# Layer 0's attention and MLP modulation on ScalarE and GpSimd instead of in 32-column strips of TensorE

## The chip, the core and the metric

The kernel runs on one NeuronCore of a Trainium2 chip. A core has engines that run side by side, each through its own instructions in a fixed order: TensorE (PE in the profile, its weight loads PEld), VectorE (DVE), ScalarE (ACT), GpSimd (POOL), and SyncE (SP), which here issues nearly all DMA transfers. The metric is the device time of one launch in microseconds.

## The reference, cut to what matters

Two layers work on 512 latent tokens and 256 context tokens of width 1024. Each layer makes six modulation vectors of 1024 numbers for the latent tokens (from the condition `c`) and six for the context tokens (from `c_ctx`), with one matrix of 1024 x 6144 for each layer.

```python
def modulation(cond, w_mod, b_mod):
    m = jax.nn.silu(cond) @ w_mod + b_mod
    return m.reshape(m.shape[:-1] + (N_MOD, D_MODEL))
...
for l in range(DEPTH):                       # DEPTH = 2
    sh1, sc1, ga1, sh2, sc2, ga2 = modulation(c, w_mod[l], b_mod[l])       # latent
    csh1, ... , cga2             = modulation(c_ctx, w_mod[l], b_mod[l])   # context
    h = modulate(rmsnorm(x, norm1_g[l]), sh1, sc1)
    z = h @ w_in[l]                          # q, k, v, u, g
    attn = softmax(q k^T) v ;  gm = gelu(u) * (w_s @ layernorm(gelu(g)) + b_s)
    x = x + ga1 * (concat(attn, gm) @ w_out[l])
    x = x + ga2 * (square(relu(modulate(rmsnorm(x, norm2_g[l]), sh2, sc2) @ w_ff1[l])) @ w_ff2[l])
```

The context stream does the same with its own vectors, but in the last layer only its keys and values are needed. So of layer 1 the context needs only the first two vectors (shift and scale of the first norm).

## The kernel before, in words

All numbers are float32. Large products are made of three matmuls on rounded halves: `split` (L206) makes `hi` on ACT and the rest `lo` as source minus `hi` on DVE or POOL, and each product takes hi x hi, hi x lo and lo x hi. The activations lie feature-major in units `A0..A7`, `B0..B6`, `C0`, `C1`, weights come as blocks of 128 x 1024 in a ring that SP loads ahead (`pump`, L224, four blocks live).

The 6144 modulation columns of a layer are 12 chunks `j` of 512 columns: chunks 0 to 3 are shift and scale of the first norm, 4 and 5 the gate of the output projection, 6 to 9 shift and scale of the second norm, 10 and 11 the gate of the MLP. Two ways of making a chunk exist:

- `mod_chunk` (L315): eight float32 matmuls of 32 x 512 (L326), whose results stand in four 32-row strips of a PSUM bank `pb`. DVE turns the bank in 32 x 32 blocks (L334), and four small matmuls with a selection matrix (L339) add the strips. Layer 0 uses it for all its chunks: 0 to 3 at the start, 4 to 11 in the attention. Its weights go through the common ring (tile `hi`).
- `mod_wide` (L347): for each of 8 rows of blocks, and for both conditions, ACT multiplies 128 x 512 weights by a number for each partition (L368, into a tile `s`), and POOL adds the product to an accumulator (L369, two inputs in SBUF). After eight rows DVE turns (L380) and sums (L381) the accumulators, and four small matmuls (L386) finish. Layer 1's chunks are made so while layer 0's MLP runs. The weights come through two buffers of the tile `k`.

Tiles `s` are shared: the ring `tsm` (L184) has three buffers for products, for GELU's work tiles, for squares and for others.

One emission clock (`Flow`, L48) counts TensorE time in ns while the program is written: `defer` puts work off to a time of this clock, `fill` and `step` put in pieces of filler. A scheduler then orders each engine's instructions by its own estimate, except in regions marked as written by hand (the start on PE and DVE, layer 0's MLP on DVE and ACT).

A layer runs: projections of u, g, k, v and q (`PLAN`, L116), attention, output projection, second norm, MLP. In a projection each PSUM bank is drained by ACT and DVE: `qk` (L588) squares on ACT, multiplies by the rotary tables on DVE (L597, L601, PSUM in), adds (L602), makes 1/rms in nine small DVE instructions (L277 to L287) and scales (L608). `stack` splits the result (L613 on ACT, L614 on POOL for layer 0). In attention a tile of 128 queries takes scores on PE (`pa<-B,B`, L203), a maximum on DVE (L825), the exponential on ACT (L828), a reciprocal on DVE (L830), a copy on POOL (L833), turns on PE (L844), halves on ACT and DVE (L846, L847) and the product with V on PE (`pb<-A,B`). After each of layer 0's 48 tiles one piece of filler is emitted: first the eight pieces of chunks 4 and 5, then, as `FILL0` (L114) says, 16 pieces of the output projection of the gated half (o, `pb<-A,hi`) and 24 pieces of chunks 6 to 11 (m). `make_gm` (L770) must have split that half before (L774 on ACT, L775 on DVE for two tiles and on POOL for two).

## Time and profile before

| | |
|---|---|
| median of 3 runs | 1533.01 us (1531.71 to 1535.66) |
| span of the profiled execution | 1530.9 us, from the first to the last instruction; 2.1 us less than the median of the runs, which stands for its own time, as the profiled execution's whole time is not given apart |
| PE busy | 1484.1 us, 97% |
| DVE, ACT, POOL busy | 957.4, 682.6, 402.0 us |
| instructions | 22786 |

On this time axis layer 0's projections lie at 42 to 177 us, its attention at 177 to 351, its MLP at 436 to 905, layer 1 behind. A row of the view by stretches gives, for each engine, busy time and number of instructions, then granted clock of TensorE, share of the DMA engines and GB/s. In a row of groups stand busy us and mean ns of one, then the idle time of the engine just before, with what ended it. A profile's fp32 matmul counts as two or more records, so a strip matmul is two.

### The profile page before, as it was taken

The page shows a single profiled execution, that of the slowest core. Times are in us where ns is not written, and L with a number is a line of the kernel's source. Part 1 is how long each engine was busy: PE and PEld are TensorE (multiplying, and loading weights), DVE is VectorE, ACT ScalarE, POOL GpSimd, SP SyncE. Part 2 cuts the span into 40 slices and gives each one's busy share as a digit, 9 for nine tenths or more (in the row PEclk, how much of TensorE's full clock was granted, in tenths as well). Part 3 has the DMA queues.
Part 4 walks back from the last instruction along what each step waited for, and adds up shares of the span by engine and source line. Part 5 has one row for each costly group of instructions (what it writes and reads, how often), then busy time and mean ns, then how long its engine had stood idle before and what let it go on. Part 6 is the DMA issues. An engine that isn't in the chain of part 4 may idle for free.

```text
span 1530.9 us, 22786 instructions
## 1 busy us (share of the span) xinstructions
PE 1484.1 (97%) x8804; PEld 1321.5 (86%) x8804; DVE 957.4 (63%) x1874; ACT 682.6 (45%) x1142; POOL 402.0 (26%) x362
## 2 busy tenths in 40 slices
PE   6999899999999999999999999998999999999998
PEld 2899686779899999999999998996889888888887
DVE  5868966776855555555555547988796644444443
ACT  3542355564545453545444424535784433322221
POOL 0112320023244545545454603035213000000000
PEclk9999999999999999999999999999999999999999
DMA  9221324321134333333333321221101333332332
GB/s 359 67 74 48 119 91 152 110 83 56 62 108 122 113 123 126 111 118 106 124 109 124 98 68 56 86 80 44 41 1 56 97 96 97 98 97 97 96 98 79
DMA packets 49948, 148.83 MB, mean 97 GB/s; under 512 B 5424, under 2 KB 6832, under 8 KB 49840
## 3 DMA queue, kind: packets, MB, share of 16 engines
q1 hardware_dynamic: 49264, 146.46, 29.9%
q8 instruction: 69, 1.13, 0.3%
q10 hardware_dynamic: 576, 0.92, 0.2%
q14 instruction: 39, 0.32, 0.1%
HBM read 145.26 MB, written 2.10 MB: 96 GB/s over the span
## 4 chain that ended last, share of the span: by engine, by line
PE 82%; DVE 12%; DMA 2%; ACT 2%; issue 1%; POOL 0%; SPq 0%; ACTq 0%; POOLq 0%; DVEq 0%
PE pa L203 51%; PE pb L203 21%; PE pt L844 3%; PE pt L203 3%; PE pb L326 2%; DVE lo L208 1%; DMA X<-in_xT 1%; DMA C<-in_w_mod 1%; DVE X L784 1%; DMA A<-in_w_mod 1%; DVE m L277 1%; PE pt L626 1%; DVE B L961 1%; ACT hi L207 1%; PE pb L865 0%
## 5 line engine op out<-in xcount | busy, mean ns | idle before, releaser
L203 PE MATMUL pa<-A,hi 128*128 128x384 f32 (+2 forms) x1696 | 449.2, 347 | 1.7 <-ACT w L954 0.6
L207 ACT CAST hi<-raw 128x1024 fp32r<-128x1024 f32 x171 | 179.5, 1050 | 409.9 <-PE pa L203 326.3
L208 DVE TENSOR_TENSOR lo<-raw,hi 128x1024 fp32r<-128x1024 f32 x155 | 202.7, 1308 | 215.8 <-ACT hi L207 212.4
L203 PEld LDWEIGHTS pa<-A,hi 128*128 128x128 f32 x1696 | 304.7, 188 | 25.9 <-ACT w L954 1.8
L369 POOL TENSOR_TENSOR C<-C,s 128x512 f32<-128x512 f32 x168 | 240.5, 1463 | 245.0 <-ACT s L368 244.8
L203 PE MATMUL pa<-A,lo 128*128 128x384 f32 (+2 forms) x848 | 293.4, 347 | 1.1 <-DVE lo L208 1.1
L203 PE MATMUL pa<-B,hi 128*128 128x384 f32 (+1 forms) x900 | 246.4, 356 | 4.4 <-DVE X L784 4.4
L203 PEld LDWEIGHTS pa<-B,hi 128*128 128x128 f32 x900 | 162.9, 188 | 21.5 <-DVE X L784 9.2
L784 DVE SCALAR_TENSOR_TENSOR X<-pa,modT,X 128x384 f32<-128x384 f32 (+1 forms) x168 | 88.0, 547 | 143.0 <-PE pa L203 143.0
L203 PEld LDWEIGHTS pa<-A,lo 128*128 128x128 f32 x848 | 159.3, 188 | 12.0 <-DVE lo L208 1.3
L203 PE MATMUL pa<-B,lo 128*128 128x384 f32 (+1 forms) x450 | 158.1, 353 | 0.0
L203 PE MATMUL pb<-B,hi 128*128 128x256 f32 (+2 forms) x600 | 152.3, 340 | 0.4 <-DVE X L784 0.4
L368 ACT ACTIVATE s<-k,silu 128x512 f32<-128x512 f32 x168 | 114.3, 716 | 49.4 <-DMA k<-in_w_mod 27.3
L203 PE MATMUL pb<-hi,A 128*128 128x256 f32 x672 | 126.1, 285 | 0.0
L784 DVE SCALAR_TENSOR_TENSOR X<-pb,modT,X 128x512 f32<-128x512 f32 (+3 forms) x116 | 69.1, 602 | 75.8 <-PE pb L203 75.3
L203 PEld LDWEIGHTS pb<-B,hi 128*128 128x128 f32 x600 | 104.0, 189 | 11.6 <-DVE X L784 1.0
L203 PEld LDWEIGHTS pb<-hi,A 128*128 128x128 f32 x672 | 106.1, 191 | 0.2 <-issue 0.2
L203 PE MATMUL pb<-B,lo 128*128 128x256 f32 (+2 forms) x300 | 101.5, 338 | 0.0
L203 PE MATMUL pb<-lo,A 128*128 128x256 f32 x336 | 95.3, 284 | 0.0
L203 PEld LDWEIGHTS pa<-B,lo 128*128 128x128 f32 x450 | 84.4, 188 | 5.8
L847 DVE TENSOR_TENSOR A<-pt,A 128x384 fp32r<-128x384 f32 (+1 forms) x144 | 73.6, 535 | 16.4 <-ACT A L846 14.4
L846 ACT CAST A<-pt 128x384 fp32r<-128x384 f32 (+1 forms) x144 | 64.6, 469 | 43.3 <-PE pt L844 39.5
(169 smaller groups left out, 2300.3 us busy)
## 6 DMA issues: line engine op xcount, KB each, us to landing
raw<-in_w_ff SPq DMA_DIRECT2D x128, 512.0 KB, 3.5
k<-in_w_mod SPq DMA_DIRECT2D x96, 256.0 KB, 3.0
hi<-in_w_mod SPq DMA_DIRECT2D x32, 512.0 KB, 3.6
raw<-in_w_tok SPq DMA_DIRECT2D x19, 512.0 KB, 3.5
raw<-in_w_out SPq DMA_DIRECT2D x16, 512.0 KB, 3.5
A<-in_w_mod SPq DMA_DIRECT2D x8, 512.0 KB, 9.9
raw<-in_w_u SPq DMA_DIRECT2D x8, 512.0 KB, 3.5
B<-in_w_mod SPq DMA_DIRECT2D x6, 512.0 KB, 10.2
```

The costliest lines, as they stand in the source:

```text
L203: pe.matmul(out, a, b, start=start, stop=stop)
L207: act.copy(hi, src)
L208: (eng or vec).tensor_tensor(out=lo, in0=src, in1=hi.bitcast(F32), op=ALU.subtract)
L277: vec.tensor_scalar(yi, v.bitcast(I32), -0.5, 1595932665.0, op0=ALU.mult, op1=ALU.add)
L326: pe.matmul(ps[q:q + 32, :], S32[:, k, :], w[:, k2 * 512:(k2 + 1) * 512], start=k < ns, stop=k >= KT - ns)
L368: act.activation(p, w, AF.Copy, scale=s)
L369: pool_e.tensor_tensor(out=a, in0=a, in1=p, op=ALU.add)
L626: pe.transpose(p[:, o:o + 128], stk[:, t, hh, c0:c0 + 128].bitcast(F32), ident)
L784: vec.scalar_tensor_tensor(out=xs, in0=src[:, s - off:e - off], scalar=modT[l][:, i * 8 + m, cond:cond + 1], in1=xs, op0=ALU.mult, op1=ALU ...
L844: pe.transpose(tp_[:, (kt - k0) * 128:(kt - k0) * 128 + 128], p[:, kt * 128:kt * 128 + 128], ident)
L846: act.copy(pth[:, k0:k0 + step, d], src)
L847: vec.tensor_tensor(out=ptl[:, k0:k0 + step, d], in0=src, in1=pth[:, k0:k0 + step, d].bitcast(F32), op=ALU.subtract)
```

## The change

Chunks 4 to 11 of layer 0 are no longer made by `mod_chunk` but by `mod_wide`, as a background generator that the emission clock advances by one row of blocks for every 3600 ns of its time, from the start of layer 0's projections. `mod_wide` gets four buffers for the weights of its own (`mr`, three loaded ahead) and an accumulator of its own (`macc`); it gives up its turn after every row, and no longer between the last sum and the turning. For layer 1 the chunks 4 to 11 are made for the latent condition alone. `FILL0` now tells after which of the 48 attention tiles a piece of output projection is emitted. The lines of the changed kernel stand ten lower than before (L193 for L203, L198 for L208), and `mod_wide`'s are L345 (load), L361 (product), L362 (sum), L371 and L372 (turn, sum).

```diff
@@ PAR
-       "PV1": 9800.0, "NC": 21600.0, "REL": 4100.0, "NP": 14, ...
+       "PV1": 9800.0, "NC": 21600.0, "REL": 4100.0, "BG": 3600.0, "NP": 14, ...
@@ Flow.tick
         while self.todo and self.todo[0][0] <= self.vt:
             self.todo.pop(0)[2]()
+        while self.bg is not None and self.bgt <= self.vt:
+            self.bgt += next(self.bg, 1e9)
-FILL0 = "oooooooommmommmmmmmmmommmmommmommmomoomo"
+FILL0 = "1101101101101101" + "01000100010001000100100100100100"
@@ block_order: the blocks of chunks 4 to 11 leave the common stream
-        if l == 0:
-            o += mod(4) + mod(5)
...
+        o += [("out", l, w, nb) for w in range(2) for nb in range(4)]
@@ mod_wide
-        raw = tk([128, 2, 512], F32)
+        raws = [const.tile([128, 512], F32, tag=f"mr{i}", name=nm("mr")) for i in range(4)] if not mraw else mraw
...
+        for i in range(3):
+            load(i)
+        for i, (j, k) in enumerate(steps):
+            conds = range(2 if l == 0 or j < 4 else 1)
+            if k == 0:
+                acc = const.tile([128, 2, 512], F32, tag="macc", name=nm("macc"))
+            load(i + 3)
+            w = mraw[i % 4]
+            for cond in conds:
+                a, s = acc[:, cond, :], sc[:, k, cond:cond + 1]
+                if k == 0:
+                    act.activation(a, w, AF.Copy, scale=s)
+                else:
+                    p = tsm([128, 512])
+                    act.activation(p, w, AF.Copy, scale=s)
+                    pool_e.tensor_tensor(out=a, in0=a, in1=p, op=ALU.add)
+            if k < KT - 1:
+                yield period
+                continue
...
@@ attention
-                                fl.step()
+                                if FILL0[nt[0]] == "1":
+                                    fl.step()
+                                nt[0] += 1
...
-                fl.fillers = [mods((4, 5)), mixed(fl.fillers[0], mods((6, 7, 8, 9, 10, 11))), fl.fillers[1]]
@@ main
+    fl.bg, fl.bgt = mod_wide(0, range(4, 12), PAR["BG"]), fl.vt
```

The order of the instructions moves as follows at three places.

POOL, in layer 0's q projections. `C` is the gate path that takes the mixed values (L743, L738 in the new kernel), `k` the low half of a stacked query (L614, L609), `A` the low half of the gated values, `macc` an accumulator of a chunk, `lo` the low half of output weights. Before:

```order
L743 TENSOR_TENSOR C_125_566<-s_1663,C_125_566 128x2x256
L614 TENSOR_TENSOR k_1769<-w_1617,k_1769 128x8x64
L743 TENSOR_TENSOR C_125_566<-s_1753,C_125_566 128x2x256
L614 TENSOR_TENSOR k_1857<-w_1707,k_1857 128x8x64
L614 TENSOR_TENSOR k_1947<-w_1800,k_1947 128x8x64
L614 TENSOR_TENSOR k_2035<-w_1890,k_2035 128x8x64
L775 TENSOR_TENSOR A_418_2375<-C_125_566,A_418_2375 128x768
```

Now, from the second of these rows on:

```order
L609 TENSOR_TENSOR k_1992<-w_1826,k_1992 128x8x64
L362 TENSOR_TENSOR macc_1816<-macc_1816,s_1996 128x512
L738 TENSOR_TENSOR C_130_577<-s_1976,C_130_577 128x2x256
L362 TENSOR_TENSOR macc_1816<-macc_1816,s_1999 128x512
L362 TENSOR_TENSOR macc_1816<-macc_1816,s_2027 128x512
L362 TENSOR_TENSOR macc_1816<-macc_1816,s_2030 128x512
L198 TENSOR_TENSOR lo_2093<-raw_2090,hi_2092 128x1024
L198 TENSOR_TENSOR lo_2099<-raw_2096,hi_2098 128x1024
L362 TENSOR_TENSOR macc_1816<-macc_1816,s_2106 128x512
L609 TENSOR_TENSOR k_2102<-w_1930,k_2102 128x8x64
```

Between two splits of queries POOL now has five sums and two splits of output weights, which stood behind the first attention tiles before. In all, 58 sums stand ahead of the split of the gated values (`A`) and 54 behind it.

ACT, at the same place: `hi` is a weight's high half, `B` a turned query, `s<-pb` the square of a q bank (L591, now L586), `s<-mr` a product of the modulation. Before:

```order
L613 CAST k_1769<-w_1617 128x8x64
L591 ACTIVATE s_1703<-pb_1637 128x512
L591 ACTIVATE s_1796<-pb_1727 128x512
L627 CAST B_249_1611<-pt_1829 128x2x256
L627 CAST B_250_1612<-pt_1835 128x2x256
L613 CAST k_1857<-w_1707 128x8x64
```

Now:

```order
L608 CAST k_1992<-w_1826 128x8x64
L361 ACTIVATE s_1996<-mr_504,silu 128x512
L361 ACTIVATE s_1999<-mr_504,silu 128x512
L361 ACTIVATE s_2027<-mr_501,silu 128x512
L361 ACTIVATE s_2030<-mr_501,silu 128x512
L197 CAST hi_2092<-raw_2090 128x1024
L586 ACTIVATE s_2033<-pb_1950 128x512
L197 CAST hi_2098<-raw_2096 128x1024
L361 ACTIVATE s_2106<-mr_502,silu 128x512
L622 CAST B_311_1820<-pt_2066 128x2x256
```

Four products and a weight's half stand between a query's split and the next square. In all, 69 products stand ahead of the first exponential of layer 0's attention, and 61 among its exponentials (two of these are layer 1's first).

PE, in the attention of the latent tokens: scores (`pa<-B,B`), turns (`pt<-c,w`), strips (`pb<-hi,S`) and the product with V (`pb<-A,B`). Before:

```order
L203 MATMUL pa_3297<-B_108_487,B_250_1612 128x256
L326 MATMUL pb_3261<-hi_3133,S_86 32x512 x2
L844 MATMUL pt_3335<-c_70,w_3241 128x128 x3
L844 MATMUL pt_3341<-c_70,w_3241 128x128 x3
L203 MATMUL pa_3347<-B_107_486,B_284_1884 128x512
L203 MATMUL pa_3347<-B_108_487,B_284_1884 128x512
L203 MATMUL pa_3347<-B_107_486,B_284_1884 128x256
L203 MATMUL pa_3347<-B_108_487,B_284_1884 128x256
L326 MATMUL pb_3261<-hi_3203,S_86 32x512
```

Now:

```order
L193 MATMUL pa_3740<-B_108_487,B_312_1821 128x512
L840 MATMUL pt_3727<-c_70,w_3619 128x128 x3
L193 MATMUL pa_3740<-B_107_486,B_312_1821 128x256
L193 MATMUL pa_3740<-B_108_487,B_312_1821 128x256
L193 MATMUL pb_3761<-A_770_3686,B_109_488 128x256
L193 MATMUL pa_3791<-B_107_486,B_360_2136 128x512
L193 MATMUL pa_3791<-B_108_487,B_360_2136 128x512
```

The strips are gone (64 strip matmuls less in the program, 32 of the start are left), and attention's own matmuls stand next to each other. The four selection matmuls of a chunk are as many as before.

More of the change, by code (lines that the diff above doesn't have):

```diff
@@ L56, in __init__ @@
         self.busy = False
+        self.bg = None
+        self.bgt = 0.0
     def defer(self, delay, fn):
@@ L318, in mod_chunk @@
         ps = pb()
-        ns = PAR["NS"] if j < 4 else 4
+        ns = PAR["NS"]
         rows = ns * 32
@@ L1004, in layer @@
             K1.append(consts(l + 1))
-        wide = None if last else mod_wide(l + 1)
+        wide = None if last else mod_wide(l + 1, range(12))
         def more(n=1):
```

86 lines of the change are left out of this document (25 added, 61 removed), and 2 rows, old and new, of the table PAR.

## The prediction

> **What bounds the kernel now.** I read the page's engine shares and chain of waits first, then the view by stretches for the stages that the change touches, then the chain and the strip matmuls within the attention.
>
> ```profile
> PE 1484.1 (97%) x8804; PEld 1321.5 (86%) x8804; DVE 957.4 (63%) x1874; ACT 682.6 (45%) x1142; POOL 402.0 (26%) x362
> PE 82%; DVE 12%; DMA 2%; ACT 2%; issue 1%; POOL 0%; SPq 0%; ACTq 0%; POOLq 0%; DVEq 0%
> ```
>
> TensorE bounds the whole. But the shares are an average, and the change takes TensorE time in one stage and gives DVE, ACT and POOL time in two. The rows below are layer 0's projections, its attention and its MLP (length, then busy time of PE, PEld, DVE, ACT, POOL).
>
> ```profile
> 42.00:177.00 135.00, 132.87 (x994) 129.35 (x996) 108.97 (x346) 56.05 (x97) 24.87 (x22) 0.97 0.20 61
> 177.00:351.00 174.00, 165.04 (x1050) 122.68 (x1047) 121.50 (x278) 97.07 (x226) 36.36 (x59) 0.98 0.36 118
> 436.00:905.00 469.00, 464.56 (x2722) 455.51 (x2722) 251.34 (x340) 219.58 (x295) 236.64 (x166) 1.00 0.37 114
> ```
>
> In the projections PE is busy 98% and DVE is next with 81%: 26 us of slack. In the attention PE is busy 95%, DVE 70%, ACT 56%. In the MLP PE has 4.4 us of idle time in 469.
>
> **What is removed: strips on PE.** The strips' records within the attention, and the chain of the same stretch:
>
> ```profile
> 177.00:351.00 174.00, 36.23 (x128) 4.77 (x124) 0.98 0.36 118
> by line: PE pb L203 34.8%; PE pb L326 18.0%; PE pa L203 15.4%; PE pt L844 14.6%; issue 2.8%; DVE A L775 2.6%; PE pb L865 2.6%; DVE A L847 1.5%; ACT w L828 1.3%; DVE m L825 1.0%; PE pt L626 1.0%; PE pt L339 0.8%; DVE B L208 0.8%; DVE w L608
> ```
>
> The 64 matmuls have 36.2 us of records, which overlap their neighbours, and 18.0% of 174 us, 31.3 us, on the chain. I take 31.3 us as what the attention's PE is relieved of. None of it lies in the projections.
>
> **What is added.** Layer 0 gets 128 products on ACT and 112 sums on POOL, and DVE turns and sums 16 accumulators where it turned 8 banks.
>
> ```profile
> L368 ACT ACTIVATE s<-k,silu 128x512 f32<-128x512 f32 x168 | 114.3, 716 | 49.4 <-DMA k<-in_w_mod 27.3 <-POOL C L369 21.8
> L369 POOL TENSOR_TENSOR C<-C,s x168: 1272/1294/2328, 409.2 to 876.1; 128x512 f32<-128x512 f32 x168
> L380 DVE STREAM_TRANSPOSE s<-C 128x512 f32<-128x512 f32 x24 | 16.8, 701 | 0.0
> L381 DVE TENSOR_REDUCE m<-s 128x16 f32<-128x512 f32 x24 | 16.4, 685 | 0.8
> ```
>
> By the order, 58 sums, 69 products and 4 chunks' endings fall into the projections, 54, 61 and 4 into the attention. In the projections ACT goes to 56.1 + 69 x 0.716 = 105.5 us and POOL to 24.9 + 58 x 1.294 = 99.9 us, both under 135: they hide beside PE if nobody waits for their order. DVE gets 8 x (0.701 + 0.685) = 11.1 us: also within its 26 us.
>
> **The term that the busy times do not show.** GpSimd's sums take two inputs from SBUF. The timeline of the q projections has such POOL instructions, and DVE's beside them:
>
> ```profile
> 150.27 1.28 POOL L743 TENSOR_TENSOR C<-s,C 128x512 f32<-128x512 f32 x1 [2.46 <-DVE m L285]
> 153.23 1.31 POOL L614 TENSOR_TENSOR k<-w,k 128x512 fp32r<-128x512 f32 x1 [1.68 <-ACT k L613]
> 158.19 1.28 POOL L743 TENSOR_TENSOR C<-s,C 128x512 f32<-128x512 f32 x1 [3.66 <-DVE m L285]
> 150.30 1.27 DVE L286 TENSOR_TENSOR m<-m,m 128x8 f32<-128x8 f32 x1
> 154.28 0.68 DVE L597 TENSOR_TENSOR w<-pb,G 128x512 f32<-128x512 f32 x1
> 157.07 0.17 DVE L283 TENSOR_TENSOR m<-m 128x8 f32<-128x8 f32 x1
> 158.23 1.27 DVE L286 TENSOR_TENSOR m<-m,m 128x8 f32<-128x8 f32 x1
> ```
>
> An instruction of 8 elements that takes 0.17 us alone takes 1.27 us when POOL began just before it, and ends with POOL's (150.30 + 1.27 and 150.27 + 1.28; the same at 158). L597, which reads PSUM, runs its 0.68 us through POOL's 153.23 to 154.54. So what waits is a DVE instruction with all inputs in SBUF. The q stage by groups gives the price of one POOL instruction:
>
> ```profile
> 123.00:177.00 54.00, 53.61 (x448) 52.85 (x449) 48.22 (x158) 19.04 (x31) 13.74 (x11) 1.00 0.15 43
> L608 DVE TENSOR_TENSOR w<-w,m 128x512 f32<-128x512 f32 x5 | 5.0, 994 | 0.2
> L286 DVE TENSOR_TENSOR m<-m,m 128x8 f32<-128x8 f32 x5 | 3.0, 608 | 0.1
> L606 DVE TENSOR_SCALAR m<-m 128x8 f32<-128x8 f32 x5 | 2.9, 582 | 0.0
> L277 DVE TENSOR_SCALAR m<-m 128x8 int32<-128x8 int32 x5 | 1.9, 383 | 0.0
> L718 DVE TENSOR_SCALAR m<-mv 128x4 f32<-128x4 f32 x3 | 1.6, 537 | 0.1
> L602 DVE TENSOR_TENSOR w<-w,s 128x512 f32<-128x512 f32 x4 | 2.7, 686 | 0.0
> L284 DVE TENSOR_TENSOR m<-m,m 128x8 f32<-128x8 f32 x5 | 0.8, 162 | 0.1
> ```
>
> Against the undisturbed rows (L602 0.69 us, L284 0.16 us) the excess is 5 x 0.31 (L608) + 5 x 0.45 (L286) + 5 x 0.42 (L606) + 5 x 0.22 (L277) + 3 x 0.37 (L718) = 8.1 us, for 11 POOL instructions in this stretch: 0.73 us each. The low bound is the MLP, where DVE has few such instructions:
>
> ```profile
> L208 DVE TENSOR_TENSOR lo<-raw,hi 128x1024 fp32r<-128x1024 f32 x55 | 79.8, 1450 | 102.3 <-ACT hi L207 102.3
> L961 DVE TENSOR_TENSOR B<-w,B 128x768 fp32r<-128x768 f32 x24 | 36.7, 1528 | 0.8
> L960 DVE TENSOR_TENSOR w<-w 128x768 f32<-128x768 f32 x26 | 24.9, 956 | 7.9 <-ACT B L959 7.2 <-ACT C L959 0.7
> L208 DVE TENSOR_TENSOR lo<-raw,hi 128x1024 fp32r<-128x1024 f32 x61 | 74.8, 1227 | 94.3 <-ACT hi L207 91.2
> ```
>
> The first three are of the MLP, the last of layer 1's, where POOL is idle. 55 x 0.22 + 24 x 0.57 (L961 against L960 of the same size) = 26 us over 166 POOL instructions: 0.16 us each. The projections are the stage of the 0.73, so I lean to it and take 0.6 us for each of the 58 sums, 34.8 us. DVE then needs 109.0 + 11.1 + 34.8 = 154.9 us in a stage of 135; with 3 us in which it must wait all the same (half of the 5.8 us that it is idle in the q stretch, an estimate) the stage becomes 158: **+23 us**. Behind a blocked DVE instruction stand the reads of PSUM that free the banks `pb` and `pt`, and PE waits for those. Bounds: at 0.16 us the sum is 132.4, under 135, so 0; at 0.73 it is 165.4, +30.
>
> [...] Were every sum to block DVE for its full 1.294 us, 58 of them would cost 75 us and the stage 63 us; the measured 0.73 us says that a part meets DVE in something else.
>
> **The attention's new bound.** PE falls to about 174 - 31 = 143 us. ACT rises to 97.1 + 61 x 0.716 = 140.8, POOL to 36.4 + 54 x 1.294 = 106.3, DVE to 121.5 + 11.1 - 5.7 (eight turns of L334) = 126.9. ACT becomes as tight as PE, and it runs in order: exponentials wait for DVE's maximum, and a product put ahead of one delays it.
>
> ```profile
> L334 DVE STREAM_TRANSPOSE s<-pb 128x512 f32<-128x512 f32 x6 | 4.3, 713 | 5.2 <-PE pb L326 5.2
> 177.00:187.00 10.00, 4.33 (x29) 1.79 (x25) 9.79 (x19) 2.64 (x6) 5.49 (x4) 0.94 0.93 322
> 178.66 4.52 DVE A L775 x2
> ACT w L828 <- DVE m L825: 19.4, 14, 6.1
> ```
>
> The first 10 us belong to DVE (9.8 busy; the split of the gated values L775 stalls PE) and stay; PE's new first filler needs just that split. In the other 164 us ACT has 138.2 us to do. At 92% use, as its 19.4 us of waits for the maximum shrink but do not vanish, this takes 150 us, the stage 160: **-14 us**. Bounds: PE's -31 if ACT never holds it up, and -1 at 85% use. Output projection that moves between this stage and the one behind changes no sum.
>
> **The MLP** loses 64 products and 56 sums of layer 1's context half, and loads three blocks ahead instead of one, which ends most of ACT's 27.3 us of waits on `k`.
>
> ```profile
> PE pa L203 <- DVE X L784: 4.4, 5, 1.2
> ```
>
> But PE was idle only 4.4 us there, so at most that is won; I take **-2.5 us**. DVE now meets a chunk's turning right behind its last two sums, at worst 2 x 1.3 us for each of 12 chunks; PE's two banks `pa` and the spare ones cover that (the wait above is 1.2 us at its longest), and without this cover it would be +3. SP gets 64 loads of 256 KB for 32 of 512 KB; each waits for ACT to free its buffer, and loads of output weights stand behind. With DMA at 36% and three blocks ahead I cost it at nothing.
>
> **Sum.** 1530.9 + 23 - 14 - 2.5 = 1537.4 us of span; the median of the runs is 2.1 us above the span, so **1539.5**, which I give as 1539.
>
> **The rivals.**
> Faster: the sums land where DVE waits or reads PSUM, at 0.3 us each the projections lose 3 us (109.0 + 11.1 + 17.4 + 3 = 140.5 would be 5; some backlog passes into the attention), ACT is used at 96% (138.2 / 0.96 + 10 = 154, -20), and the MLP gives 2.5: 1533 - 19.5 = 1513.5. For it: in the MLP the same pair costs 0.16 us a sum, and the projections' first 81 us have more slack than the q stretch. Against it: the q rows. It decides below 0.41 us a sum, where the projections lose under 12 us.
> Even: at 0.49 us a sum the loss is 16.5 us and cancels 14 + 2.5: 1533.
> Slower still: the three `s` buffers tie ACT to POOL, so that exponentials stand behind products that wait for POOL's sums; the attention wins nothing: 1533 + 23 - 2.5 = 1553.5. For it: ACT's 21.8 us of waits on POOL in the MLP at 50% POOL load; against it: POOL has 106 of 160 us.
> That the strips stay is excluded by the order.
>
> **How the numbers follow.** Forecast 0.38 (its own range 1537.7 to 1548), slower still 0.11, even 0.15, faster 0.36. About 0.3%, 4.6 us, is what a measurement of this kernel can tell from no change: slower 0.49, same 0.15, faster 0.36. The range reaches from 2 us below the faster case to just above the slowest: 1511 to 1556.
>
> **What would show it.** Right: the projections longer by some 20 us, DVE over 95% busy there, mean durations of L277 to L287, L602 and L608 (ten lines higher in the new numbering) two to three times those above, PE waiting for DVE's reads of `pb`; the attention shorter with ACT the busiest after PE. Wrong: small DVE instructions still near 0.2 us and a stage of 135 to 140 us, which gives the faster case; or an attention that stays at 174 us with ACT waiting for POOL.

## The result, and the profile after

The changed kernel takes 1584.57 us (median of 4 runs, 1581.16 to 1585.87) against 1532.36 before: a ratio of 1.0333, 95% interval 1.0315 to 1.0352. It is slower by 52 us; 1539 was predicted, with a range up to 1556. The profiled execution has a span of 1582.0 us against 1530.9.

The page's engine shares and chain of waits of the changed kernel:

```profile
PE 1473.7 (93%) x8676; PEld 1334.7 (84%) x8676; DVE 1000.8 (63%) x1882; ACT 717.8 (45%) x1206; POOL 465.0 (29%) x418
PE 69%; DVE 18%; ACT 7%; DMA 2%; issue 2%; POOL 2%; SPq 0%; ACTq 0%; POOLq 0%; DVEq 0%
```

PE has 10 us less to do, as intended, and has lost 13 points of the chain, 6 of them to DVE and 5 to ACT. To see where, both executions are divided at the same three instructions: the first exponential (attention begins), the first ReLU (MLP begins), and POOL's first scaling of layer 1. In the view by line the second number behind the colon is the first start in us; first the kernel before, then the changed one.

```profile
L828 ACT ACTIVATE w<-pa,m x80: 473/903/919, 186.0 to 1142.4; 128x768 f32<-128x768 f32 x64, 128x256 f32<-128x256 f32 x16
L954 ACT ACTIVATE w<-pa x72: 363/591/815, 394.2 to 1505.7; 128x512 f32<-128x512 f32 x32, 128x768 f32<-128x768 f32 x28, 128x256 f32<-128x256 f32 x12
L608 POOL TENSOR_TENSOR w<-w,m x7: 613/1042/1362, 960.7 to 1054.4; 128x512 f32<-128x512 f32 x4, 128x256 f32<-128x256 f32 x3
```

```profile
L824 ACT ACTIVATE w<-pa,m x80: 465/903/943, 248.4 to 1193.0; 128x768 f32<-128x768 f32 x64, 128x256 f32<-128x256 f32 x16
L942 ACT ACTIVATE w<-pa x72: 364/590/815, 434.2 to 1556.7; 128x512 f32<-128x512 f32 x32, 128x768 f32<-128x768 f32 x28, 128x256 f32<-128x256 f32 x12
L603 POOL TENSOR_TENSOR w<-w,m x7: 615/1043/1361, 1012.0 to 1106.0; 128x512 f32<-128x512 f32 x4, 128x256 f32<-128x256 f32 x3
```

| us | to the first exponential | attention and output projection | MLP | rest |
|---|---|---|---|---|
| before | 186.0 | 208.2 | 566.5 | 570.2 |
| changed | 248.4 | 185.8 | 577.8 | 570.0 |
| difference | +62.4 | -22.4 | +11.3 | -0.2 |
| predicted | +23 | -14 | -2.5 | 0 |

The attention won more than forecast. The projections lost almost three times the forecast, and the MLP, which was to win a little, lost 11 us. Some work changed sides at the first mark: about 8.5 us of output projection run ahead of the first exponential now, and 4.1 us of strips and their load no longer do, so some 4 us of the first two differences are no gain or loss. The stretches of the changed kernel (busy PE, PEld, DVE, ACT, POOL, granted clock):

```profile
42.00:123.00 81.00, 69.02 (x450) 65.21 (x451) 60.22 (x145) 49.82 (x86) 37.62 (x32) 0.92 0.33 105
123.00:184.00 61.00, 45.14 (x317) 43.65 (x316) 48.57 (x140) 27.72 (x44) 32.24 (x26) 0.84 0.30 96
184.00:240.00 56.00, 37.88 (x266) 36.72 (x265) 54.63 (x82) 26.64 (x41) 40.66 (x28) 0.77 0.21 63
248.40:434.20 185.80, 169.50 (x1121) 150.76 (x1121) 147.09 (x324) 143.41 (x311) 104.59 (x120) 0.98 0.21 66
```

Only from 184 to 240 us is DVE full (98%). From 42 to 184 us it is busy 77%, PE 80%, and still both fall behind: no engine is full there. What that looks like at its worst, in the q projections, first on DVE, then on POOL:

```profile
205.76 2.29 DVE L267 TENSOR_SCALAR m<-m 128x8 int32<-128x8 int32 x1
208.08 1.18 DVE L270 TENSOR_TENSOR m<-m 128x8 f32<-128x8 f32 x1
209.30 1.19 DVE L271 SCALAR_TENSOR_TENSOR m<-m,m 128x8 f32<-128x8 f32 x1
210.52 1.20 DVE L272 SCALAR_TENSOR_TENSOR m<-m,m 128x8 f32<-128x8 f32 x1
211.75 0.17 DVE L273 TENSOR_TENSOR m<-m 128x8 f32<-128x8 f32 x1
...
212.56 1.27 DVE L277 SCALAR_TENSOR_TENSOR m<-m,m 128x8 f32<-128x8 f32 x1
```

```profile
205.65 2.37 POOL L198 TENSOR_TENSOR lo<-raw,hi 128x1024 fp32r<-128x1024 f32 x1
207.97 1.27 POOL L362 TENSOR_TENSOR macc<-macc,s 128x512 f32<-128x512 f32 x1
209.19 1.28 POOL L609 TENSOR_TENSOR k<-w,k 128x512 fp32r<-128x512 f32 x1
210.41 1.29 POOL L362 TENSOR_TENSOR macc<-macc,s 128x512 f32<-128x512 f32 x1
212.53 1.28 POOL L362 TENSOR_TENSOR macc<-macc,s 128x512 f32<-128x512 f32 x1 [0.83 <-ACT s L361]
```

Each small DVE instruction of 1/rms ends with the POOL instruction that began just before it. While POOL is idle (211.7 to 212.5) they take 0.17 us. POOL's row is dense now, so a chain of small instructions moves at POOL's step (1.18 to 1.27 us each in these rows). The view of PE's waits from 42 us to the first exponential of the changed kernel (us, times, longest):

```profile
PE pt L375 <- DVE m L372: 15.8, 3, 8.6
PE pb L193 <- DVE A L770: 8.9, 1, 8.9
PE pt L621 <- POOL k L609: 7.0, 3, 3.2
PE pa L193 <- DVE C L675: 4.1, 2, 3.0
```

Before, the largest total in that list was 3.1 us. The first row is new: PE, in order, stands at a chunk's selection matmul until DVE has summed the accumulator.

### The profile page after: what moved, and what is told of

Its sections match the earlier page's. It is cut to its first block, busy times and chain, and to the rows that moved or that the text cites. A ratio compares the mean times of both kernels' runs of the same rounds, so it can differ in the third digit from the quotient of the medians.

```text
span 1582.0 us, 22749 instructions
## 1 busy us (share of the span) xinstructions
PE 1473.7 (93%) x8676; PEld 1334.7 (84%) x8676; DVE 1000.8 (63%) x1882; ACT 717.8 (45%) x1206; POOL 465.0 (29%) x418
## 4 chain that ended last, share of the span: by engine, by line
PE 69%; DVE 18%; ACT 7%; DMA 2%; issue 2%; POOL 2%; SPq 0%; ACTq 0%; POOLq 0%; DVEq 0%
PE pa L193 46%; PE pb L193 17%; PE pt L840 2%; PE pt L193 2%; ACT w L824 1%; ACT hi L197 1%; POOL macc L362 1%; DVE m L267 1%; DVE B L949 1%; DVE lo L198 1%; ACT s L361 1%; DVE X L780 1%; DMA X<-in_xT 1%; DVE m L271 1%; ACT A L842 1%
## 5 line engine op out<-in xcount | busy, mean ns | idle before, releaser
L193 PE MATMUL pa<-A,hi 128*128 128x384 f32 (+2 forms) x1696 | 452.1, 349 | 9.0 <-DVE C L675 4.1
L362 POOL TENSOR_TENSOR macc<-macc,s 128x512 f32<-128x512 f32 x224 | 307.1, 1388 | 369.3 <-ACT s L361 364.6
L198 DVE TENSOR_TENSOR lo<-raw,hi 128x1024 fp32r<-128x1024 f32 x155 | 192.9, 1244 | 226.0 <-ACT hi L197 222.8
L193 PEld LDWEIGHTS pa<-A,hi 128*128 128x128 f32 x1696 | 306.0, 189 | 34.7 <-DVE C L675 4.5
L193 PE MATMUL pa<-A,lo 128*128 128x384 f32 (+2 forms) x848 | 294.5, 348 | 1.3 <-DVE lo L198 1.3
L193 PE MATMUL pa<-B,hi 128*128 128x384 f32 (+1 forms) x900 | 246.1, 356 | 5.5 <-DVE X L780 5.4
L193 PEld LDWEIGHTS pa<-B,hi 128*128 128x128 f32 x900 | 163.2, 188 | 22.5 <-DVE X L780 10.8
L361 ACT ACTIVATE s<-mr,silu 128x512 f32<-128x512 f32 x224 | 155.4, 719 | 42.6 <-POOL macc L362 27.0
L193 PEld LDWEIGHTS pa<-A,lo 128*128 128x128 f32 x848 | 160.0, 189 | 12.7 <-DVE lo L198 1.7
L193 PE MATMUL pa<-B,lo 128*128 128x384 f32 (+1 forms) x450 | 158.3, 354 | 0.0
L193 PE MATMUL pb<-B,hi 128*128 128x256 f32 (+2 forms) x600 | 152.8, 341 | 1.1 <-DVE X L780 0.7
L193 PE MATMUL pb<-hi,A 128*128 128x256 f32 x672 | 134.5, 296 | 5.4 <-DVE w L600 1.9
L193 PEld LDWEIGHTS pb<-hi,A 128*128 128x128 f32 x672 | 112.7, 203 | 6.4 <-DVE w L600 2.1
L193 PEld LDWEIGHTS pb<-B,hi 128*128 128x128 f32 x600 | 104.2, 189 | 12.7 <-DVE X L780 1.0
L193 PE MATMUL pb<-B,lo 128*128 128x256 f32 (+2 forms) x300 | 101.7, 339 | 0.0
L193 PE MATMUL pb<-A,hi 128*128 128x512 f32 (+2 forms) x288 | 87.9, 383 | 12.9 <-DVE A L770 8.9
L193 PE MATMUL pb<-lo,A 128*128 128x256 f32 x336 | 99.2, 295 | 0.6 <-DVE lo L198 0.6
L422 POOL TENSOR_TENSOR acc<-acc,s 128x256 f32<-128x256 f32 (+1 forms) x43 | 46.8, 1089 | 174.3 <-ACT s L420 173.0
L193 PEld LDWEIGHTS pa<-B,lo 128*128 128x128 f32 x450 | 84.4, 188 | 6.0
```

The source lines that it names most:

```text
L193: pe.matmul(out, a, b, start=start, stop=stop)
L198: (eng or vec).tensor_tensor(out=lo, in0=src, in1=hi.bitcast(F32), op=ALU.subtract)
L361: act.activation(p, w, AF.Copy, scale=s)
L362: pool_e.tensor_tensor(out=a, in0=a, in1=p, op=ALU.add)
L422: eng.tensor_tensor(out=self.acc, in0=self.acc, in1=sq, op=ALU.add)
```

## The experiments

**Leave the sums out.** Layer 0's products, loads and endings stay.

```diff
-                    pool_e.tensor_tensor(out=a, in0=a, in1=p, op=ALU.add)
+                    if l:
+                        pool_e.tensor_tensor(out=a, in0=a, in1=p, op=ALU.add)
```

> The changed kernel with layer 0's 112 sums on GpSimd left out (58 in the projections, 54 in the attention); products, loads, turnings and selection matmuls stay, so the gates and the second norm's shift and scale of layer 0 are computed from one row of blocks and are not the reference's. Theory 'lock' (each sum keeps DVE from its SBUF-only instructions) and theory 'queues' (in-order ACT, POOL and PE stand behind the sums and the three s buffers) both say that the first exponential comes back from 248 us to 186 to 197 us and the total to 1520 to 1535 us; small DVE instructions of the rsqrt (L267 to L277) back under 0.25 us mean. Rival 'products' (ACT's 69 products ahead of the first exponential, their loads and the chunk endings are what costs): the first exponential stays past 220 us and the total past 1555 us.

Measured: 1531.46 us, ratio 0.9988 (0.9976 to 0.9999); first exponential at 205.8 us.

```profile
L825 ACT ACTIVATE w<-pa,m x80: 462/902/947, 205.8 to 1143.2; 128x768 f32<-128x768 f32 x64, 128x256 f32<-128x256 f32 x16
```

248.4 - 205.8 = 42.6 us for the 58 sums ahead of it: the stage loses 0.73 us for each. But it does not come back whole: 19.8 us stay. The total is that of before, to 2 us: as it stands, this change would have won about 0.1% even with sums that cost nothing. The total came out as expected. The first exponential did not: the 186 to 197 us were missed, and the rival's 220 us too. Nor did all small instructions fall under 0.25 us: `L267` on 128x8 still has a mean of 0.97 us, beside POOL's other work (2.32 us once, beside a split of output weights).

**Replace each sum by a copy** with one input, so that order and buffers stay.

```diff
-                    pool_e.tensor_tensor(out=a, in0=a, in1=p, op=ALU.add)
+                    if l:
+                        pool_e.tensor_tensor(out=a, in0=a, in1=p, op=ALU.add)
+                    else:
+                        pool_e.tensor_copy(a, p)
```

> The changed kernel with each of layer 0's 112 two-input sums on GpSimd replaced by a one-input copy of the product into the accumulator (so these modulation values are wrong sums); order, buffers and the tie between ACT, POOL and the endings stay. Theory 'lock', if only two-input instructions lock: small DVE instructions back to 0.2 us, first exponential at 190 to 205 us, total 1525 to 1540 us. Theory 'queues': POOL still stands in the chain with 58 instructions, first exponential at 215 to 245 us, total above 1555 us. If copies lock as well: DVE instructions stretched to the copy's length, and the loss falls in proportion to the length of a copy against 1.3 us.

Measured: 1548.61 us, ratio 1.0101 (1.0072 to 1.0131).

```profile
L827 ACT ACTIVATE w<-pa,m x80: 458/902/942, 220.8 to 1158.5; 128x768 f32<-128x768 f32 x64, 128x256 f32<-128x256 f32 x16
L365 POOL COPY macc<-s 128x512 f32<-128x512 f32 x59 | 38.4, 661 | 67.9 <-ACT s L361 67.9
```

220.8 - 205.8 = 15.0 us for copies of 0.66 us, against 42.6 us for sums of 1.31: the loss falls with POOL's time, faster than in proportion, which would leave 21.5 us. Small DVE instructions beside copies take 0.51 to 0.57 us: copies block too. The first exponential alone does not tell theory 'lock' from the rival 'queues', whose 215 to 245 us it also meets (the total misses it). DVE's own busy time does. The stage from 42 us to the first exponential (busy PE, PEld, DVE, ACT, POOL) before, without sums, with copies, and in the changed kernel:

```profile
42.00:186.00 144.00, 136.83 (x1018) 130.78 (x1018) 117.77 (x360) 58.12 (x100) 30.22 (x24) 0.98 0.25 78
42.00:205.80 163.80, 147.59 (x1058) 141.99 (x1058) 132.91 (x381) 103.28 (x173) 39.00 (x28) 0.93 0.36 113
42.00:220.80 178.80, 153.37 (x1060) 147.51 (x1060) 145.67 (x381) 104.74 (x174) 76.80 (x87) 0.90 0.32 103
42.00:248.40 206.40, 158.04 (x1056) 151.45 (x1057) 169.83 (x380) 105.39 (x172) 111.52 (x86) 0.84 0.29 91
```

With the same instructions DVE is busy 36.9 us longer beside the sums (0.64 us for each) and 12.8 us longer beside the copies. DVE's waits for other engines stand in its idle time (9.7 us on ACT's `s` of L670 in this stretch of the changed kernel), and the 36.9 and 12.8 us are longer instructions; so the blocking makes most of the 42.6 and 15.0 us. DVE's idle time did not shrink to make room: 30.9 us without sums, 36.6 with them.

**The price by itself.** Rows of ten DVE instructions behind the end of the kernel before, alone or beside ten POOL instructions of 128x512; one of the eight rows in code:

```diff
+        sum_ = lambda: pool_e.tensor_tensor(out=acc, in0=acc, in1=p, op=ALU.add)
+        one_ = lambda: pool_e.tensor_copy(acc, p)
+        tt = lambda: vec.tensor_tensor(out=m0, in0=m0, in1=m1, op=ALU.add)
+        for pool_op, dve_op in ((None, tt), (sum_, tt), (one_, tt), ...):
```

> The kernel before with short rows of DVE and POOL instructions put behind its last output, some 100 us of them; its answer is unchanged. Ten dependent DVE additions of 128x8 alone; beside ten POOL sums of 128x512 (two SBUF inputs); beside ten POOL copies (one input); then tensor_scalar, an addition that reads PSUM, a reduction, and an addition of 128x512, each beside ten POOL sums. Theory 'lock': alone about 0.07 to 0.2 us, beside sums 1.2 us each, one per sum, for the SBUF-only tensor_tensor and tensor_scalar; the PSUM reader and the reduction keep their length. Rival (a sum blocks DVE for about 0.7 us on average whatever DVE does, or slows only the first instruction that meets it): most of the ten stay under 0.3 us.

The timeline of DVE, where a row with x10 is ten instructions and its time from the first's start to the last's end: the additions of 128x8 alone, beside sums, beside copies; tensor_scalar beside sums; an addition that reads PSUM, and a reduction, beside sums; additions of 128x512 alone and beside sums.

```profile
1528.67 1.97 DVE L1117 TENSOR_TENSOR m<-m,m 128x8 f32<-128x8 f32 x10
1531.07 6.79 DVE L1117 TENSOR_TENSOR m<-m,m 128x8 f32<-128x8 f32 x10
1544.98 3.52 DVE L1117 TENSOR_TENSOR m<-m,m 128x8 f32<-128x8 f32 x10
1552.32 6.81 DVE L1118 TENSOR_SCALAR m<-m 128x8 f32<-128x8 f32 x10
1566.24 1.97 DVE L1119 TENSOR_TENSOR m<-pt,m 128x8 f32<-128x8 f32 x10
1580.12 7.17 DVE L1120 TENSOR_REDUCE m<-s 128x8 f32<-128x512 f32 x10
1593.88 7.22 DVE L1121 TENSOR_TENSOR w<-w,s 128x512 f32<-128x512 f32 x10
1601.30 15.69 DVE L1121 TENSOR_TENSOR w<-w,s 128x512 f32<-128x512 f32 x10
```

And POOL's row beside the last of these, against its undisturbed one beside the reductions:

```profile
1580.23 13.35 POOL L1115 TENSOR_TENSOR w<-w,s 128x512 f32<-128x512 f32 x10 [0.55 <-DVE s L1123]
1601.53 16.57 POOL L1115 TENSOR_TENSOR w<-w,s 128x512 f32<-128x512 f32 x10 [7.96 <-DVE s L1123]
```

Beside sums ten small additions need 6.79 us in place of 1.97, beside copies 3.52; the additions with a PSUM input are not touched (1.97), nor are the reductions (7.17 us for ten, where `L593` has 0.68 for one). 6.79 us is the time of about five sums (13.35 us for ten), and the first two small instructions took 1.39 us together, about one sum: so, by this estimate, two pass for each sum (the expectation had one). A sum that met this chain cost it 4.82 / 5 = 0.96 us, and one that met the PSUM readers cost nothing; the 0.64 us of DVE's time above lie between, as the projections have instructions of both kinds. The copies' row loses 1.55 us, a third of the sums' 4.82, as the stage lost a third (15.0 of 42.6). With additions of 128x512 on both sides each waits for the other: DVE's ten take 2.2 times as long, POOL's 1.24 times.

For the case that every sum blocks DVE for its whole 1.294 us the prediction had worked out +63 us for the stage. The stage did lose 62.4, but only 42.6 of it through the sums, so the agreement is partly chance.

**Put the endings off on PE.** The selection matmuls and the storing come 9000 ns of the emission clock later (abridged).

```diff
-            mod_store(l, j, p4.rearrange("p b a -> p a b"), nc_)
+            if l == 0:
+                fl.defer(PAR["SEL"], fin)      # fin: the four matmuls and mod_store
+            else:
+                fin()
```

> The changed kernel with each of layer 0's eight chunk endings on PE (four selection matmuls and the storing) put off by 9000 ns of the emission clock after the turning, nothing else. Theory 'queues': PE's 15.8 us of waits on the accumulators' column sums in the projections go, and with them 12 to 25 us of the stage; total 1560 to 1573 us. Theory 'lock': DVE has been late for everything else too, PE's waits move to the banks that DVE reads, the stage loses under 6 us; total 1578 to 1586 us.

Measured: 1580.59 us, ratio 1.0310 (1.0280 to 1.0340); first exponential 246.2. PE's waits on the column sums fell from 15.8 to 4.1 us and came back elsewhere, a little at many places (on the split of the gated values 11.3 for 8.9, on POOL's query split 8.7 for 7.0): all its listed waits add up to 50 us in both. PE had been waiting for a late DVE, not for a badly placed matmul.

**One DVE instruction for product and sum** (abridged; the first row's products go to DVE as well).

```diff
+                elif l == 0:
+                    vec.scalar_tensor_tensor(out=a, in0=w, scalar=s, in1=a, op0=ALU.mult, op1=ALU.add)
```

> The changed kernel with each product and sum of layer 0 made by one DVE instruction (accumulator plus weights times a number for each partition) in place of ACT's product and POOL's sum; endings and layer 1 untouched. A DVE instruction of this size takes 0.69 us. Theory 'a sum costs DVE about 0.73 us wherever it is made' (42.6 us for 58 sums in the projections): DVE gets about 64 x 0.69 = 44 us there for the 42.6 it loses to the lock, ACT and POOL are free; first exponential at 225 to 250 us, total 1570 to 1590 us. Rival 'it is the order across three engines, not DVE's time' (each small instruction waiting behind a POOL instruction that waits for ACT): first exponential at 195 to 215 us, total below 1555 us.

Measured: 1581.84 us, ratio 1.0318 (1.0297 to 1.0339). The first exponential comes at 226.9 us: 21.5 us earlier than with ACT and POOL, although DVE carries the whole work. By the first exponential alone the first theory's 225 us hold at their edge. The attention then has to carry the same on DVE and is 205.2 us instead of 185.8, so the total is the same.

```profile
42.00:226.90 184.90, 153.46 (x1070) 145.40 (x1070) 176.31 (x458) 61.94 (x104) 44.19 (x29) 0.93 0.33 107
```

DVE is busy 6.5 us longer than in the changed kernel, and the stage is still 21.5 us shorter. Against the run without sums DVE has 43.4 us more to do, and the stage is only 21.1 us longer: DVE's idle time falls from 30.9 to 8.6 us. ACT's products are gone there too, which by itself moves the mark by 0.5 us (the next experiment). So work of DVE's own went into its idle time by about half; the 36.9 us by which the sums stretched its instructions did not at all.

**What are the remaining 20 us of the projections?** Three removals more, on top of the left-out sums: the products; the endings, with and without the products; and POOL's splits of output weights, which go to DVE.

```diff
                 else:
+                    if l == 0:
+                        continue
                     p = tsm([128, 512])
```

> The changed kernel with layer 0's products of the rows of blocks 1 to 7 left out together with their sums (the first row's 16 products, all loads, turnings and endings stay; so these modulation values are of one row of blocks alone). Without sums but with products the first exponential stands at 205.8 us, 19.8 us later than before. Theory 'ACT in order' (products stand ahead of squares, GELU's steps and halves on ACT, which is busy 95% from 64 to 76 us): first exponential at 188 to 195 us. Rival 'endings and weight splits' (PE's 7.0 us of waits on column sums and two splits of output weights of 2.5 us on POOL make the rest): 198 to 206 us.

```diff
+            if l == 0:
+                mod_store(l, j, acc[:, :, 0:4].rearrange("p b a -> p a b"), nc_)
+                yield period
+                continue
```

> As the run without layer 0's products and sums, and with layer 0's eight chunk endings left out as well: no turning, no column sums, no selection matmuls, the stored values are read from the accumulator's first columns (they are not the modulation). Loads and the first row's 16 products stay. Theory 'endings' (eight DVE instructions of 0.7 us ahead of the first exponential, and PE in order behind each: 9.7 us of PE's waits): first exponential from 206.3 to 188 to 196 us. Rival 'loads and weight splits': it stays at 200 to 206 us.

> The changed kernel with layer 0's sums left out and its eight chunk endings (turning, column sums, selection matmuls) left out too; the products stay and pace the loads. The stored values are read from the first row's products and are not the modulation. With sums alone left out the fifth sum of squares of the q projections stands at 188.7 us, 17.6 us later than before (171.0). Theory 'endings': 173 to 181 us. Rival 'products and loads': 183 to 190 us.

```diff
-       "WP": ['out1', 'out0']
+       "WP": ['out1']
```

> As the run without layer 0's products and sums, with layer 0's output weights split on DVE (1.22 us) in place of POOL (2.48 us). Theory 'weight splits' (two of them stand between the queries' splits on POOL now, and block DVE's small instructions for 2.4 us each): first exponential from 206.3 to 196 to 202 us. Rival 'endings': 203 to 209 us.

The first exponential is a coarse mark, since some output projection now runs ahead of it. So here is also DVE's fifth sum of squares of the q banks; before, changed, sums left out:

```profile
171.04 0.68 DVE L593 TENSOR_REDUCE m<-s 128x8 f32<-128x512 f32 x1
```

```profile
225.85 0.68 DVE L588 TENSOR_REDUCE m<-s 128x8 f32<-128x512 f32 x1
```

```profile
188.66 0.67 DVE L589 TENSOR_REDUCE m<-s 128x8 f32<-128x512 f32 x1
```

| left out in layer 0 | total, us (ratio, interval) | first exponential | fifth sum of squares, later than before |
|---|---|---|---|
| nothing (the change) | 1584.57 | 248.4 | +54.8 |
| sums | 1531.46 | 205.8 | +17.6 |
| sums, products | 1529.17 (0.9974, 0.9963 to 0.9985) | 206.3 | +16.8 |
| sums, endings | 1526.94 (0.9957, 0.9941 to 0.9972) | 207.3 | +15.6 |
| sums, products, endings | 1524.08 (0.9939, 0.9919 to 0.9959) | 204.5 | +16.4 |
| sums, products; weight splits on DVE | 1524.41 (0.9941, 0.9921 to 0.9961) | 205.5 | +13.9 |

None of the three theories holds. Each removal alone gives 1 to 3 us in the projections, and some bring waits of their own: without products the loads run ahead (the DMA share from 42 to 123 us is 0.76, in the changed kernel 0.33), and without endings as well ACT waits 20.2 us for them. Up to the fifth sum of squares without sums, 10.1 of the 17.6 us are idle time of PE and 7.5 us its busy time, at a granted clock of 0.93 for 0.97 before. What is common to all these kernels was not taken away: 38 of the 64 loads, which start ahead of the first exponential now, the first row's products, and another order of the whole stage. Where these 14 to 18 us come from stays open.

**The MLP: give up the turn again** between a chunk's last sum, its turnings and its end, for layer 1 alone.

```diff
+            if l:
+                yield                      # before the turning, and after each
```

> The changed kernel with layer 1's mod_wide giving up its turn again between a chunk's last sum, its turnings and its end, as before; layer 0 untouched. In the changed kernel the stretch from the MLP's first relu to layer 1's first POOL scaling is 577.8 us, 11.3 us longer than before (566.5), though it has 64 products and 56 sums less. Theory 'endings' (DVE and ACT, ordered by hand there, stand at a turning that waits for its last sums): the stretch comes back to 563 to 568 us, total 1569 to 1576 us. Rival 'accumulator and loads' (the four small buffers, 256 KB loads, the accumulator's place): it stays above 574 us, total above 1580 us.

For layer 1 the edit also drops the turn after a chunk's first row and the one at its end, as before; the parts were not tried singly.

Measured: 1571.21 us, ratio 1.0256 (1.0240 to 1.0271); the MLP goes from 577.8 to 567.5 us. PE's waits in the whole MLP, first in the changed kernel, then here:

```profile
PE pa L193 <- DVE X L780: 7.5, 12, 0.9
PE pt L375 <- DVE m L372: 6.0, 6, 1.1
```

```profile
PE pa L193 <- DVE X L786: 5.1, 6, 0.9
```

PE's idle time goes from 16.1 to 6.8 us, which is 9.3 of the 10.3 us. Without these turns PE, in its order, stood six times at a chunk's selection matmuls until DVE had summed the accumulator, and waited longer for DVE's sums into `X`; with the turns the first wait is gone and the second near the 4.4 us of before. ACT waits at the next chunk's first product, which writes the same accumulator, in both:

```profile
ACT macc L358 <- DVE s L371: 62.8, 11, 8.2
```

```profile
ACT macc L358 <- DVE s L374: 59.8, 10, 11.2
```

Before it was 53.4 us. It hardly changes with the turns, so it is not what made the MLP longer.

**Layer 1's context half alone**, on the kernel before:

```diff
-                for cond in range(2):
+                for cond in range(2 if j < 4 else 1):
```

> The kernel before with one part of the change: layer 1's chunks 4 to 11 for the latent condition alone (64 products and 56 sums less; the answer needs only these). Theory 'relief' of the prediction: -2.5 us, 1528.5 to 1531.5 us. Rival 'PE sets the MLP and nothing is won': within 1 us of before, 1531.5 to 1534 us.

Measured: 1532.90 us, ratio 1.0000 (0.9991 to 1.0010), MLP 567.5 us. 64 products and 56 sums less are worth nothing: they were hidden.

**The attention alone.** Layer 0's last chunks by products and sums that start with the attention, the others by strips as before, the turns given up as before. Only the number of chunks, their pace and the order of the fillers differ. The core of it, for two chunks:

```diff
+FILL0 = "1" * 48                            # a piece of filler after every tile
+NSTRIP = 10                                 # chunks 4 to 9 by strips
+MIX0 = "oooooooommommommommommommommommo"
+            fl.fillers = [mods((4, 5)), mixed(fl.fillers[0], mods(range(6, NSTRIP))), fl.fillers[1]]
+            fl.bg, fl.bgt = mod_wide(0, range(NSTRIP, 12), PAR["BG"]), fl.vt
```

> A version between the two: layer 0's chunks 4 to 7 by strips in the attention as before, 8 to 11 by products and sums that start with the attention (none in the projections), layer 1 latent alone with the turns given up as before. In the changed kernel the attention with 61 products, 54 sums and no strips was 22.4 us shorter than before. Theory 'place' (the change is bad only where DVE and ACT have no slack beside PE): projections at 186 us to the first exponential, attention with half the strips (15.6 us of 31.3 on PE's chain) 7 to 18 us shorter, total 1514 to 1526 us. Rival 'no slack in the attention either' (the sums delay maxima, halves and drains as in the projections): attention no shorter, total 1530 to 1545 us.

> As the version between, with two chunks (10 and 11) by products and sums in the attention and 4 to 9 by strips, one row of blocks for every 7200 ns of the emission clock. Theory 'place': 7.8 us of strips go from PE, total 1522 to 1528 us. Rival 'no slack in the attention either': 1530 to 1538 us.

> The version with chunks 8 to 11 by products and sums in the attention (which was only 3.9 us shorter there, 204.3 us for 208.2, with PE waiting 8.5 and 5.3 us for exponentials), now one row of blocks for every 5400 ns of the emission clock in place of 3600, and a piece of filler after every tile. Theory 'pace' (64 products within 57 exponentials crowd ACT; two chunks at 7200 ns gained 12.8 us): attention at 190 to 198 us, total 1512 to 1521 us. Rival 'amount' (four chunks are more than ACT can take beside PE): 200 us and more, total 1526 us and above.

> Chunks 9 to 11 by products and sums in the attention, one row of blocks for every 5400 ns, 4 to 8 by strips, layer 1 as in the versions before it. Theory 'pace': between two chunks (195.4 us of attention) and what four would give, 190 to 196 us, total 1514 to 1521 us. Rival 'amount' (ACT is full with two): 196 to 204 us, total 1521 to 1530 us.

> The version with two chunks in the attention, but with none: chunks 4 to 11 by strips, output projection and strips in that version's order, layer 1 as there. Theory 'chunks' (the two chunks made the gain): total 1529 to 1536 us. Rival 'order of the fillers': total 1518 to 1525 us.

> Chunk 11 alone by products and sums in the attention, 4 to 10 by strips, one row of blocks for every 7200 ns. Theory 'chunks': half of two chunks' gain, 1524 to 1529 us. Rival 'order of the fillers': 1518 to 1524 us, as two chunks.

> Chunks 10 and 11 by products and sums in the attention with one row of blocks for every 5400 ns in place of 7200 (1520.3 us). Theory 'amount' (two chunks fit whatever the pace): 1517 to 1524 us. Rival 'pace' (ACT crowded): 1524 to 1531 us.

| chunks made so, one row each | total, us | ratio and interval | attention and output projection, us |
|---|---|---|---|
| 0 | 1534.84 | 1.0009 (1.0000 to 1.0019) | 212.3 |
| 1, 7200 ns | 1529.85 | 0.9979 (0.9968 to 0.9990) | 205.3 |
| 2, 7200 ns | 1520.29 | 0.9924 (0.9907 to 0.9940) | 195.4 |
| 2, 5400 ns | 1523.06 | 0.9938 (0.9922 to 0.9955) | 197.6 |
| 3, 5400 ns | 1524.02 | 0.9941 (0.9926 to 0.9956) | 198.8 |
| 4, 5400 ns | 1531.89 | 0.9991 (0.9981 to 1.0000) | 207.2 |
| 4, 3600 ns, filler mostly after two tiles of three | 1530.38 | 0.9985 (0.9975 to 0.9994) | 204.3 |

The projections stay at 185 to 188 us in all of them and the MLP at 567.5. The stretch from first exponential to first ReLU with no, two, three and four chunks:

```profile
185.40:397.70 212.30, 206.72 (x1285) 161.01 (x1286) 141.69 (x321) 112.97 (x253) 46.07 (x69) 0.97 0.27 89
```

```profile
184.80:380.20 195.40, 191.16 (x1254) 158.29 (x1255) 143.51 (x327) 130.06 (x285) 81.36 (x97) 0.98 0.30 97
```

```profile
187.70:386.50 198.80, 187.92 (x1238) 157.16 (x1239) 144.99 (x330) 139.15 (x302) 98.21 (x111) 0.98 0.29 95
```

```profile
186.60:393.80 207.20, 189.32 (x1221) 161.46 (x1221) 149.99 (x333) 149.61 (x317) 115.25 (x125) 0.95 0.28 91
```

In these profiles two chunks take 16.9 us off the stretch, of which PE's own time is 15.6; PE idles 4 to 6 us in both. (The profiled execution without chunks was the slowest of its ten and the one with two the fastest of its four; the medians differ by 14.6 us.) The third takes 3.2 us more off PE, and its idle time goes to 10.9; with the fourth it is 17.9. So the place was right and the amount decides: two chunks fit beside PE, ACT at 67% and DVE at 73%, a third adds nothing that can be told from noise, and the fourth takes the gain away. The expectation 'place' was surpassed with two chunks and missed with four at 3600 ns (1530.38 for at most 1526); 'amount' held in all three runs, 'chunks' with none, and missed by 0.85 us with one. The version with two is 12 us faster than before and beats both kernels. Its 7.3 us for each chunk (14.6 / 2) are more than a chunk's 31.3 / 8 = 3.9 us of strips. In the two profiles PE's strips alone take 13.2 us less (35.1 and 21.9), so 3.9 is probably too low for a chunk; the rest the runs do not explain. The theory 'pace' fell: with three and four chunks its ranges were missed. Whether pace does anything is not shown: with four, 3600 and 5400 ns gave 0.9985 and 0.9991, with two, 7200 and 5400 ns gave 0.9924 and 0.9938, and both pairs of intervals overlap.

## Why the prediction was wrong, step by step

- **What bounds the kernel:** right for the kernel before. In the changed one PE's share of the chain falls from 82 to 69%, and from 184 to 240 us DVE is the full engine.
- **GpSimd blocks VectorE:** that POOL's sums hold up DVE's instructions with all inputs in SBUF was right for additions and `tensor_scalar` (6.79 and 6.81 us for ten, in place of 1.97 for the additions), too wide for reductions (7.17 us for ten beside sums). Why the two engines wait for each other, no run shows. The price was right. 0.73 us a sum were read from the q stretch and 0.6 taken; DVE's busy time grew by 0.64 us a sum (36.9 / 58). That the stage lost 0.73 us a sum (42.6 / 58) is another quantity; that it is as large as the one read from the q rows may be chance.
- **From the price to the stage: this is the step that failed.** The prediction added busy times on DVE, set the sum against a stage of 135 us, and so let DVE's 26 us of idle time swallow 23 of the 45.9 us that it had added. At the full 0.73 that working still gave only +30. The runs showed that nothing is swallowed. DVE's busy time grew by 52.1 us, not far from the 45.9, but its idle time, which was to fall to 3 us, grew from 26.2 to 36.6; together that is the 62.4 us. The sums alone made the stage 42.6 us longer, 36.9 us of it on DVE. An explanation that fits, though no run follows it link by link: a blocked instruction stands in a chain (PE's bank, ACT's square, DVE's nine small instructions, ACT's half, POOL's half, PE's turn), `pb` has two banks, and DVE's idle time is time in which it waits for engines that wait for it, so a delay in the chain moves the chain. DVE's product-and-sum instructions, which stand beside that chain, did use idle time (30.9 to 8.6 us). What was to show the step right, DVE over 95% busy, came only from 184 to 240 us.
- **The signs named:** the small instructions grew, most of them more than forecast (`L277` on 128x8 from 0.35 to 0.88 us, `L285` from 0.17 to 0.97); `L602` (0.69 and 0.68 us) and `L608` (0.99 and 0.90) on 128x512 did not.
- **Products, endings and weight splits "hide beside PE":** wrong by 19.8 us at the first exponential, some 4 us of which is work that changed sides; no single one of them makes it, and its cause is open.
- **The attention, -14:** right in kind, measured -22.4, or some -18 without the work that changed sides. ACT and DVE came near to PE (143.4 and 147.1 us beside 169.5 of 185.8), but ACT was never as tight as forecast. Without sums the same stretch is 178.1 us: here 54 sums cost 7.7 us, 0.14 each, near the 0.16 that the prediction had read in the MLP.
- **The MLP, -2.5:** wrong in sign, +11.3. The prediction saw that DVE meets the turning right behind the last sums, and let PE's banks cover it. They did not: PE waited 6.0 us at the selection matmuls, which stand in its own order whatever banks are free, and 3.1 us more for sums into `X`. With the turns given back the MLP is at +1.0, and the relief that was to make it faster is 0.
- **The rivals:** "slower still" had the right sign for the wrong reason. ACT's waits on POOL through the three `s` buffers did not keep the attention from winning. The faster case needed under 0.41 us a sum, and would not have come even at 0, where the total is 1531.5.

## What to carry to other kernels

Before work is put on GpSimd beside VectorE, list VectorE's instructions with all inputs in SBUF in that stage, reductions aside: a chain of small ones moved here at the pace of GpSimd's instructions (1.18 to 1.27 us each, in place of 0.17), while VectorE was busy 77% over most of the stage. VectorE's idle time took in about half of 43.4 us of work that stood beside the chain, and nothing of 36.9 us of delays within it; where, as here, banks are few and engines wait for each other in a ring, add delays to the chain and not busy times to a sum. And give such work to the stage where PE alone is full, in an amount that leaves the others a quarter to a third of their time (ScalarE was busy 67% and VectorE 73% with two chunks): two chunks in the attention won 0.8%, eight spread over both stages lost 3.3%.

## What the runs showed of the hardware

A GpSimd copy with one SBUF input blocked DVE too, for its own shorter time (copies of 0.66 us beside small DVE instructions of 0.51 to 0.57 in the run with copies; ten additions took 3.52 us in place of 1.97 beside ten copies); and a `tensor_scalar` of 128x8 with one SBUF input was blocked like an addition with two (6.81 and 6.79 us for ten). So it was not only two-input instructions that blocked or were blocked.

Where PE was busy less, its granted clock was lower: 1.00 at 99% busy in the q stretch before (123 to 177 us), and in the changed kernel 0.92 at 85%, 0.84 at 74% and 0.77 at 68% (the three stretches from 42 to 240 us).

How much of the 62.4 us the lower clock made was not measured apart; up to the fifth sum of squares PE's busy time went from 126.9 to 144.6 us, for the same work but for a few selection matmuls.
